# Splitting the last weight group, aggregating the statistics ahead, and sharing the output between two engines at the end of a hybrid decoder step

## The chip, the core and the metric

The kernel runs on one core of one Trainium2 chip. The metric is the device time of the program in microseconds (us), from its first to its last instruction, as the median of several runs. TensorE (PE in the profile) does the matmuls, VectorE (DVE), ScalarE (ACT) and GpSimd (POOL) the elementwise work. SyncE (SP), ACT and POOL also issue transfers between HBM and the on-chip memory (SBUF). Matmul results land in PSUM, in banks of 512 f32 numbers per partition.

## The reference

One layer of a hybrid decoder on 256 prompt tokens and 32 sample tokens (8 sequences of 4), 2048 features wide, all in f32. The change touches only the end of it, the feed-forward block and the layer norm behind it:

```python
merged = jax.nn.sigmoid(m_a) * y_a + jax.nn.sigmoid(m_b) * y_b
x = layer_norm(ALPHA * x + merged @ w_o, ln1_g, ln1_b)
hid = jnp.square(jax.nn.relu(x @ w_up))
x = layer_norm(ALPHA * x + hid @ w_down, ln2_g, ln2_b)
```

`w_down` is 8192 x 2048. `layer_norm` takes mean and variance over the 2048 features of a token, then scales by `g` and adds `b`.

## The kernel before, in words

**The stream.** All large weights go through one stream of blocks. A group (`add_group`, L151) is 256 output columns by some depth; a block is 4 row tiles of 128 by 256 columns, 512 KB. For block i, SP loads it (`load`, L164), ACT rounds it to a reduced f32 form (`split_hi`, L173), DVE takes the remainder (`split_lo`, L179), and PE multiplies (`matmuls`, L186): for each row tile and each half of 128 columns three matmuls, high times high, high times low, low times high (L202 to L204), 24 in a block, with the output feature on the partitions and the 288 tokens in the free dimension.

**Order of the work.** The order is written out by hand; every engine runs its queue in that order. Iteration i of the main loop (L1287) issues in turn `split_hi(i+3)`, `split_lo(i+3)`, the functions that are due at i, `matmuls(i)` and `load(i+7)`. What is due is what a group's `evac` list puts there: its functions run at the iterations after the group's last block (L207 to L209). The weight buffers are four deep, so ACT's `split_hi(i+3)` waits until PE is done with block i-1.

**The last quarter of `w_down`.** `w_down` is taken in four quarters of depth (c = 0 to 3), each in 8 groups p of 256 columns, added to the residual `acc` (feature-major, 16 tiles k of 128 features by 288 tokens; `down_evac`, L524). In the last quarter each finished group also starts the layer norm: `out_tiles(p)` (L580), three iterations later, turns its two tiles to token-major with four PE transposes (L591; two blocks b of 128 prompt tokens), DVE takes the statistics from PSUM (L594) and writes the tile times `ln2_g` to `Y` (L140 inside `scaled`, L596). For odd p, ACT copies the sample tokens of four tiles into `cs` (L604), and a generator, returned and run one iteration later by `rest` (L535), turns that copy with one more transpose (L608) and takes its statistics (L610). `tail_rows` (L571) prepares rows of `ln2_g` and `ln2_b` in `m5` for later. The last group (p = 7) is taken up after the stream has ended.

**The end (`final`, L620).** DVE merges the records of all 16 tiles for each token block (L627), ACT takes the root (L628), small operations make the mean and the factor of every token into `R`, PE turns `R` (L637), ACT copies it to `st5` (L638). The output of 8 units (token block b, 512 features n) is `Y * rs + rank1`, where `rank1` is a matmul of `st5` with `m5` (L650); unit 0 has it from DVE instead. All 8 units are DVE operations from PSUM, each followed by a store from SP (L688). Between them runs the sample's chain: merged moments (L656), a mean over four partitions by matmul (L660), copied by ACT (L661), the variance likewise (L668, L669), then ACT scales `gs` (L674), POOL adds `bs` (L675), DVE forms `Ys`, and ACT issues its four stores (L681).

**Buffers.** PSUM holds two accumulators of two banks (`acp`) and four banks (`gp`) that `gtile` hands out.

Of the kernel before, what the change touches and what calls it, by code (L numbers as in the profile page):

```python
# [16 lines left out]
P = 128  # L17
# [21 lines left out]


def _constants():
# [31 lines left out]
    f["rowhi"] = np.isin(k, (0, 2, 3)) * 1.0  # L73
# [30 lines left out]
def hybrid_kernel(ctx: ExitStack, tc: tile.TileContext, A):  # L104
# [46 lines left out]
    def add_group(W, col0, row0, nk, acts, evac, width=NT):  # L151
        gi = dict(W=W, col0=col0, acts=acts, evac=evac, width=width)
        for j in range(nk // KB):
            blocks.append((gi, row0 + j * KB * P, j * KB, j == 0, j == nk // KB - 1))
# [9 lines left out]
    def load(i):  # L164
        if i >= len(blocks):
            return
        gi, r0, k0, _, _ = blocks[i]
        t = wp.tile([P, KB, GW], F32, tag="raw", name=nm("raw"))
        sp.dma_start(t, gi["W"][r0:r0 + KB * P, gi["col0"]:gi["col0"] + GW]
                     .rearrange("(k p) c -> p k c", p=P))  # L170
        raw[i] = t
# [14 lines left out]
    def matmuls(i):  # L186
# [7 lines left out]
        for k in range(KB):  # L194
            for t in range(2):
# [5 lines left out]
                en = last and k == KB - 1  # L201
                pe.matmul(o, wh, xh_, start=st, stop=False)  # L202
                pe.matmul(o, wh, xl_, start=False, stop=False)  # L203
                pe.matmul(o, wl, xh_, start=False, stop=en)  # L204
                if fill:
                    fill.pop(0)()
# [317 lines left out]
    def down_evac(c, p):  # L524
# [3 lines left out]
        if c == 3:  # L528
            if p == 0:
                return [f, lambda ps: None, lambda ps: out_tiles(p, ps)]  # L530
            if p == 7:
                return [lambda ps: out_tiles(p, ps)]
# [8 lines left out]
            return [f, lambda ps: None, lambda ps: hold.extend(filter(None, [out_tiles(p, ps)])), rest]  # L541
        return [f]

    def tail_consts():
# [4 lines left out]
        gps.dma_start(ph["g2"], A["ln2_g"].to_broadcast([P, D]))  # L549
        gps.dma_start(ph["b0"], A["ln2_b"][:, 0:512].to_broadcast([P, 512]))  # L550
# [7 lines left out]
    def tail_tiles():  # L558
        pl = ph["pool"]
        g4 = pl.tile([P, D + 256], F32R, tag="R4", name="g4")  # L560
        ph["m5"], ph["st5"] = g4[0:5, 0:D], g4[0:5, D:D + 256]
# [5 lines left out]
        ph["sm"] = r5[:, 4320:4352]  # L567
        sp.dma_start(r5[0:3, 0:D], A["ln2_g"].to_broadcast([3, D]))
        sp.dma_start(r5[3:5, 0:D], A["ln2_b"].to_broadcast([2, D]))

    def tail_rows(n):  # L571
        c = slice(512 * n, 512 * n + 512)
        r5, m5 = ph["r5"], ph["m5"][:, c]
        raw_, lo = r5[0:5, 0, c], r5[0:5, 1, 1536:2048]
        act.copy(m5, raw_)
        tt(lo, raw_, m5, SUB)
        dve.tensor_scalar(out=m5, in0=m5, scalar1=cst("rowhi")[0:5, 0:1], scalar2=None, op0=MUL)
        stt(m5, lo, cst("rowlo")[0:5, 0:1], m5, MUL, ADD)

    def out_tiles(p, ps):  # L580
        if p == 0:
            ph["Y"] = ap_.tile([P, 2, D], F32, tag="ao", name="Y")
        Y, Ys, bn = ph["Y"], ph["Ys"], ph["bn"]
        a = ph["acc"]
        gv = [gtile()[:, 0:256].rearrange("p (b c) -> p b c", b=2) for _ in range(2)]
        if p == 7:
            for u in range(2):
                tt(a[:, 14 + u, :], a[:, 14 + u, :], ps[:, u, 0:NT], ADD)
        for u in range(2):
            for b in range(2):  # L590
                pe.transpose(gv[u][:, b, :], a[:, 2 * p + u, b * P:(b + 1) * P], ident)  # L591
        for u in range(2):
            for b in range(2):
                dve.bn_stats(out=bn[:, b, 2 * p + u, :], in_=gv[u][:, b, :])  # L594

        def scaled():  # L596
            for u in range(2):
                c = slice(256 * p + P * u, 256 * p + P * u + P)
                tt(Y[:, :, c], gv[u], bmid(ph["g2"][:, c], 2), MUL)

        w = p // 2
        if p % 2:
            cs = ph["cs"][:, (w % 2) * P:(w % 2) * P + P]
            act.copy(cs.rearrange("p (k t) -> p k t", k=4), a[:, 4 * w:4 * w + 4, NP_:NT])  # L604

        def sample():
            g2 = gtile()[:, 0:P]
            pe.transpose(g2, cs, ident)  # L608
            yield
            dve.bn_stats(out=ph["bns"][:, w, :], in_=g2)  # L610
            tt(Ys[:, w * P:(w + 1) * P], g2, ph["gs"][:, w * P:(w + 1) * P], MUL)
        if p == 7:
            ph["rest"] = scaled, sample()
            next(ph["rest"][1])
        else:
            scaled()
            if p % 2:
                return sample()

    def final():  # L620
        Y, Ys, bn, sm = ph["Y"], ph["Ys"], ph["bn"], ph["sm"]
        scaled, sample = ph["rest"]
        mv = sm[:, 0:4].rearrange("p (b s) -> p b s", b=2)
        sd, rs, r = sm[:, 4:6], sm[:, 6:8], sm[:, 8:10]
        R = ph["pool"].tile([P, 2, 5], F32R, tag="mv", name="R")
        for b in range(2):
            dve.bn_aggr(out=mv[:, b, :], in_=bn[:, b])  # L627
        act.activation(sd, mv[:, :, 1], AF.Sqrt, bias=epsc[:, 0:1])  # L628
        act.copy(R[:, :, 3:5], bc(ones[:, 0:2], 2))
        scaled()  # L630
        dve.reciprocal(out=rs, in_=sd)
        stt(r, mv[:, :, 0], -1.0, rs, MUL, MUL)
        stt(R[:, :, 0:2], bc(mv[:, :, 0], 2), -1.0, bc(rs, 2), MUL, MUL)
        tt(R[:, :, 2], r, R[:, :, 0], SUB)
        pr = gtile()
        for b in range(2):
            pe.transpose(pr[0:5, b * P:(b + 1) * P], R[:, b, :].bitcast(F32), ident)  # L637
        act.copy(ph["st5"], pr[0:5, 0:256])  # L638
# [3 lines left out]
        stt(t0, ph["g2"][:, 0:512], r[:, 0:1], ph["b0"], MUL, ADD)  # L642
        units = [(b, n) for b in range(2) for n in range(4)]
        rank1 = {0: t0}

        def prepare(i):
            if i < 8:
                b, n = units[i]
                rank1[i] = gtile()
                pe.matmul(rank1[i], ph["st5"][:, b * P:(b + 1) * P], ph["m5"][:, 512 * n:512 * n + 512],  # L650
                          start=True, stop=True)

        # sample: four rows of the tile hold a token
        def moments():
            next(sample, None)
            dve.bn_aggr(out=mq, in_=ph["bns"])  # L656

        def mean():
            pq = gtile()
            pe.matmul(pq[:, 0:2], cst("quart"), mq, start=True, stop=True)  # L660
            act.copy(me, pq[:, 0:2])  # L661

        def deviation():
            tt(dv, mq[:, 0:1], me[:, 0:1], SUB)
            tt(dv, dv, dv, MUL)
            tt(vb, me[:, 1:2], epsc[:, 0:1], ADD)
            pq = gtile()
            pe.matmul(pq[:, 0:1], cst("quart"), dv, start=True, stop=True)  # L668
            act.activation(ds, pq[:, 0:1], AF.Sqrt, bias=vb)  # L669

        def scale():
            dve.reciprocal(out=qs, in_=ds)
            stt(ts, me[:, 0:1], -1.0, qs, MUL, MUL)
            act.mul(ph["gs"], ph["gs"], ts)  # L674
            gps.tensor_tensor(out=ph["gs"], in0=ph["gs"], in1=ph["bs"], op=ADD)  # L675

        def finish():
            stt(Ys, Ys, qs, ph["gs"], MUL, ADD)
            ys = A["y_sample"].rearrange("b t (k j f) -> (b t) k j f", j=4, f=P)
            for j in range(4):  # L680
                act.dma_start(ys[:, :, j, :], Ys[32 * j:32 * j + 32, :].rearrange("p (k f) -> p k f", k=4))  # L681

        steps = {0: moments, 1: mean, 2: deviation, 4: scale, 7: finish}
        prepare(1)
        for i, (b, n) in enumerate(units):
            c = slice(512 * n, 512 * n + 512)
            stt(Y[:, b, c], Y[:, b, c], rs[:, b:b + 1], rank1[i], MUL, ADD)
            sp.dma_start(A["y_prompt"][0, b * P:(b + 1) * P, c], Y[:, b, c])  # L688
            prepare(i + 2)
            if i in steps:  # L690
                steps[i]()

    mark["up"] = len(blocks)
    for c in range(4):
# [4 lines left out]
        for p in range(8):  # L699
            add_group(A["w_down"][0], GW * p, 2048 * c, KT, lambda: (ph["hh"], ph["hl"]), down_evac(c, p))  # L700

# [149 lines left out]
    def gdn(G):  # L851
# [29 lines left out]
        # token-major keys; squared norms of keys and queries  # L881
# [490 lines left out]
```

## Time and profile before

| | |
|---|---|
| median of 3 runs | 1725.3 us (1725.29 to 1725.32) |
| the profiled execution, first to last instruction | 1725.5 us |
| PE busy | 1701.8 us (99%) |
| PE weight loads busy | 1677.6 us (97%) |
| DVE busy | 1026.3 us (59%) |
| ACT busy | 712.0 us (41%) |
| POOL busy | 123.7 us (7%) |
| mean granted TensorE clock | 0.991 of full speed |

A timeline row gives the start in us from the span's start, the length in us, the engine, the source line, the operation, what it writes and reads, shapes and count; in brackets stands how long the engine had been idle and what released it. PEld is PE's weight load, which overlaps matmuls. An engine with a q (ACTq, SPq) is that engine's queue issuing transfers. Rows merge neighbours of one kind ("x4"), so a row's length then covers all of them.

### The profile page before, as it was taken

Reading aid. Unit: us, or ns where it says so; the run is one execution under the profiler, and the core shown is the slowest. Engines: PE = TensorE matmul, PEld = TensorE weight load, DVE = VectorE, ACT = ScalarE, POOL = GpSimd, SP = SyncE. Lnnn points to the kernel's source line nnn. Section 1 sums busy time; section 2 is a strip of 40 time slices with the busy share of each in tenths; the row PEclk is TensorE's granted clock in tenths of the full one; section 3 lists DMA queues with packets and bytes.
Section 4 is the critical chain, followed back from the end, with each engine's and each line's share of the span. In section 5 each row is a group of like instructions: output and inputs, shape, how many; then the busy total and the mean of one; then the engine's idle time right before and its main releaser. Section 6 shows DMA issues by size and latency. Waiting matters only on the chain.

```text
span 1725.5 us, 31070 instructions
## 1 busy us (share of the span) xinstructions
PE 1701.8 (99%) x13037; PEld 1677.6 (97%) x13037; DVE 1026.3 (59%) x1345; ACT 712.0 (41%) x1031; POOL 123.7 (7%) x217
## 2 busy tenths in 40 slices
PE   9999999999999999999999999999999999999997
PEld 7999889999999999999999999999999999999996
DVE  5687777577454445545778754565445654456565
ACT  4664445334443333434445433344333433344331
POOL 2221231023300000000010000000000000000000
PEclk8999999999999999999999999999999999999998
DMA  8464347435655555555575555555555555555552
GB/s 241 141 181 137 106 118 233 131 103 151 207 169 162 169 165 166 159 171 160 170 204 164 166 168 163 168 160 167 166 167 163 159 171 166 165 164 166 163 158 78
DMA packets 272296, 279.76 MB, mean 162 GB/s; under 512 B 12122, under 2 KB 267035, under 8 KB 272023
## 3 DMA queue, kind: packets, MB, share of 16 engines
q1 hardware_dynamic: 267324, 265.87, 51.7%
q0 software_dynamic: 4256, 11.65, 2.3%
q8 instruction: 102, 1.67, 0.4%
q10 hardware_dynamic: 576, 0.26, 0.1%
q14 instruction: 38, 0.31, 0.0%
HBM read 270.26 MB, written 7.48 MB: 161 GB/s over the span
## 4 chain that ended last, share of the span: by engine, by line
issue 48%; PE 47%; DVE 2%; DMA 1%; ACT 1%; SPq 0%; POOLq 0%; POOL 0%; ACTq 0%; DVEq 0%
PE acc L202 14%; PE acc L203 14%; PE acc L204 14%; PE g L986 1%; DMA g<-in_ln_b_dram 1%; PE g L995 1%; DVE w L143 1%; DMA xr<-in_x_prompt_dram 0%; ACT hi L177 0%; DVE lo L140 0%; DVE w L266 0%; PE g L769 0%; DVE w L327 0%; PE g L1169 0%; PE g L1149 0%
## 5 line engine op out<-in xcount | busy, mean ns | idle before, releaser
L140 DVE TENSOR_TENSOR lo<-raw,hi 128x1024 fp32r<-128x1024 f32 (+2 forms) x502 | 608.0, 1214 | 551.6 <-ACT hi L177 549.1
L177 ACT CAST hi<-raw 128x1024 fp32r<-128x1024 f32 (+1 forms) x498 | 517.7, 1041 | 793.3 <-PE acc L203 729.7
L202 PE MATMUL acc<-xh,hi 128*128 128x288 f32 x1408 | 423.8, 301 | 0.0
L204 PE MATMUL acc<-xh,lo 128*128 128x288 f32 x1408 | 418.0, 297 | 0.0
L203 PE MATMUL acc<-xl,hi 128*128 128x288 f32 x1408 | 417.9, 297 | 0.0
L202 PE MATMUL acc<-dh,hi 128*128 128x290 f32 x1024 | 303.9, 297 | 0.0
L203 PE MATMUL acc<-dl,hi 128*128 128x290 f32 x1024 | 303.2, 296 | 0.0
L204 PE MATMUL acc<-dh,lo 128*128 128x290 f32 x1024 | 302.8, 296 | 0.0
L204 PE MATMUL acc<-hh,lo 128*128 128x288 f32 x1024 | 302.3, 295 | 0.0
L203 PE MATMUL acc<-hl,hi 128*128 128x288 f32 x1024 | 302.3, 295 | 0.0
L202 PE MATMUL acc<-hh,hi 128*128 128x288 f32 x1024 | 302.1, 295 | 0.0
L202 PEld LDWEIGHTS acc<-xh,hi 128*128 128x128 f32 x1408 | 266.8, 189 | 4.0 <-issue 1.6
L203 PEld LDWEIGHTS acc<-xl,hi 128*128 128x128 f32 x1408 | 266.9, 190 | 0.7
L204 PEld LDWEIGHTS acc<-xh,lo 128*128 128x128 f32 x1408 | 266.8, 189 | 0.0
L202 PEld LDWEIGHTS acc<-dh,hi 128*128 128x128 f32 x1024 | 193.6, 189 | 0.1
L204 PEld LDWEIGHTS acc<-dh,lo 128*128 128x128 f32 x1024 | 193.3, 189 | 0.0
L203 PEld LDWEIGHTS acc<-dl,hi 128*128 128x128 f32 x1024 | 193.2, 189 | 0.1
L203 PEld LDWEIGHTS acc<-hl,hi 128*128 128x128 f32 x1024 | 192.5, 188 | 0.0
L204 PEld LDWEIGHTS acc<-hh,lo 128*128 128x128 f32 x1024 | 192.3, 188 | 0.0
L202 PEld LDWEIGHTS acc<-hh,hi 128*128 128x128 f32 x1024 | 192.1, 188 | 0.0
L203 PE MATMUL acc<-ml,hi 128*128 128x288 f32 x256 | 75.6, 295 | 0.0
L204 PE MATMUL acc<-mh,lo 128*128 128x288 f32 x256 | 75.6, 295 | 0.0
(385 smaller groups left out, 1625.1 us busy)
## 6 DMA issues: line engine op xcount, KB each, us to landing
raw<-in_w_in_dram SPq DMA_DIRECT2D x176, 512.0 KB, 3.7
raw<-in_w_up_dram SPq DMA_DIRECT2D x128, 512.0 KB, 3.7
raw<-in_w_down_dram SPq DMA_DIRECT2D x128, 512.0 KB, 3.6
raw<-in_w_o_dram SPq DMA_DIRECT2D x32, 512.0 KB, 3.6
raw<-in_w_a_out_dram SPq DMA_DIRECT2D x16, 512.0 KB, 3.6
raw<-in_w_b_out_dram SPq DMA_DIRECT2D x16, 512.0 KB, 3.6
S<-in_state_gdn_dram POOLq DMA_DIRECT2D x8, 512.0 KB, 8.1
out_dram<-S POOLq DMA_DIRECT2D x8, 512.0 KB, 5.5
```

The costliest lines, as they stand in the source:

```text
L140: dve.tensor_tensor(out=out, in0=a, in1=b, op=op)
L143: dve.scalar_tensor_tensor(out=out, in0=a, scalar=s, in1=b, op0=o0, op1=o1)
L177: act.copy(his[i][:, k:k + step], raw[i][:, k:k + step])
L202: pe.matmul(o, wh, xh_, start=st, stop=False)
L203: pe.matmul(o, wh, xl_, start=False, stop=False)
L204: pe.matmul(o, wl, xh_, start=False, stop=en)
L986: pe.matmul(o, kqm[:, 64 * b:64 * b + 64], S0[:, hh, b, :], start=(b == 0), stop=(b == 7))
L995: pe.matmul(out[r, q * 64:q * 64 + 64], a[r, q, :], b[r, q, :], start=True, stop=True)
```

## The change

The last group of 256 columns becomes two groups of 128 columns, whose blocks are 8 row tiles deep (the same 512 KB and 24 matmuls a block). Tile 14 is added and turned while the last group still runs, and DVE merges the records of tiles 0 to 14 there (`collect`); the end merges only that result with the record of tile 15, in `fin`. For tiles 0 to 7, ACT multiplies `acc` by `ln2_g` in place (`act.mul` in `turned`, with `g2f`, a copy of `ln2_g` with one feature on each partition), and DVE no longer writes `Y` for them. At the end PE turns these eight scaled tiles again, straight into the two accumulators in PSUM (`wide`), and adds the rank part to them by matmul; ACT scales the sum by `rs` into `Y` (`act_unit`, four of the eight units), and SP stores 1024 columns at a time. Because the sum is scaled as a whole, the rank part of these units comes from a second set of rows, so `R` has twice the columns and six rows. The other four units stay on DVE. The sample's turning, `sample_tile`, is now started inside `out_tiles` at once and only its statistics wait for the next iteration. Its four stores are issued by ACT and SP, two each.

```diff
-    def add_group(W, col0, row0, nk, acts, evac, width=NT):
-        gi = dict(W=W, col0=col0, acts=acts, evac=evac, width=width)
+    def add_group(W, col0, row0, nk, acts, evac, width=NT, cols=GW):
+        kb = KB * GW // cols
+        gi = dict(W=W, col0=col0, acts=acts, evac=evac, width=width, cols=cols, kb=kb)
...
-            return [f, lambda ps: None, lambda ps: hold.extend(filter(None, [out_tiles(p, ps)])), rest]
+            return [f, lambda ps: None, lambda ps: hold.extend(filter(None, [out_tiles(p)])), rest]
...
+    def next_to_last(ps):
+        a = ph["acc"][:, 14, :]
+        tt(a, a, ps[:, 0, 0:NT], ADD)
+
+    def collect(ps):
+        turned(14)
+        fin, bn = ph["fin"], ph["bn"]
+        for b in range(2):
+            dve.bn_aggr(out=fin[:, b, 1:3], in_=bn[:, b, 0:15])
+        dve.tensor_scalar(out=fin[:, :, 2], in0=fin[:, :, 2], scalar1=15.0 * P, scalar2=None, op0=MUL)
...
+        sp.dma_start(ph["g2f"], A["ln2_g"][:, 0:1024].rearrange("o (k p) -> p (o k)", p=P))
...
+    def turned(k, record=None):
...
+        for b in range(2):
+            pe.transpose(gv[:, b, :], a[:, k, b * P:(b + 1) * P], ident)
+        for b in range(2):
+            dve.bn_stats(out=ph["bn"][:, b, k, :] if record is None else record[:, b], in_=gv[:, b, :])
...
+        if k >= 8:
+            scaled()
+        else:
+            act.mul(a[:, k, 0:NP_], a[:, k, 0:NP_], ph["g2f"][:, k:k + 1])
+
+    def sample_tile(w):
+        a = ph["acc"]
+        cs = ph["cs"][:, (w % 2) * P:(w % 2) * P + P]
+        act.copy(cs.rearrange("p (k t) -> p k t", k=4), a[:, 4 * w:4 * w + 4, NP_:NT])
+        g2 = gtile()[:, 0:P]
+        pe.transpose(g2, cs, ident)
+        yield
+        dve.bn_stats(out=ph["bns"][:, w, :], in_=g2)
+        if w == 3:
+            yield
+        tt(ph["Ys"][:, w * P:(w + 1) * P], g2, ph["gs"][:, w * P:(w + 1) * P], MUL)
+
+    def out_tiles(p):
+        for u in range(2):
+            turned(2 * p + u)
+        if p % 2:
+            g = sample_tile(p // 2)
+            next(g)
+            return g
+
+    def final(ps):
+        a, fin, sm = ph["acc"], ph["fin"], ph["sm"]
+        tt(a[:, 15, 0:NP_], a[:, 15, 0:NP_], ps[:, 0, 0:NP_], ADD)
+        tt(a[:, 15, NP_:NT], a[:, 15, NP_:NT], ps[:, 0, NP_:NT], ADD)
+        scaled = turned(15, fin[:, :, 3:9])
+        sample = sample_tile(3)
+        next(sample)
...
+        for b in range(2):
+            dve.bn_aggr(out=mv[:, b, :], in_=fin[:, b])
+        act.activation(sd, mv[:, :, 1], AF.Sqrt, bias=epsc[:, 0:1])
...
+        for n in range(2):
+            w = acp.tile([P, 2, 512], F32, tag="acc", name=nm("acc"))
+            wide.append(w)
+            for b in range(2):
+                for k in range(4):
+                    pe.matmul(w[:, b, P * k:P * k + P], a[:, 4 * n + k, b * P:(b + 1) * P], ident,
+                              start=(k == 0), stop=False, is_transpose=True)
...
+        act.copy(ph["st5"], pr[0:6, :])
...
+        def act_unit(b, n):
+            c = slice(512 * n, 512 * n + 512)
+            act.mul(Y[:, b, c], wide[n][:, b, :], rs[:, b:b + 1])
+            if n:
+                sp.dma_start(A["y_prompt"][0, b * P:(b + 1) * P, 0:1024], Y[:, b, 0:1024])
+
+        def dve_unit(b, n, rank1):
+            c = slice(512 * n, 512 * n + 512)
+            stt(Y[:, b, c], Y[:, b, c], rs[:, b:b + 1], rank1, MUL, ADD)
+            sp.dma_start(A["y_prompt"][0, b * P:(b + 1) * P, c], Y[:, b, c])
...
+        rank(wide[0][:, 0], 0, 0, 0, False)
+        r12 = rank_tile(1, 2)
+        pq = gtile()
+        pe.matmul(pq[:, 0:2], cst("quart"), mq, start=True, stop=True)
+        act.copy(me, pq[:, 0:2])
+        rank(wide[1][:, 0], 0, 0, 1, False)
+        act_unit(0, 0)
+        dve_unit(0, 2, t0)
+        next(sample, None)
+        tt(dv, mq[:, 0:1], me[:, 0:1], SUB)
+        tt(dv, dv, dv, MUL)
...
+        pe.matmul(pq2[:, 0:1], cst("quart"), dv, start=True, stop=True)
+        rank(wide[0][:, 1], 0, 1, 0, False)
+        rank(wide[1][:, 1], 0, 1, 1, False)
+        r03 = rank_tile(0, 3)
+        act.activation(ds, pq2[:, 0:1], AF.Sqrt, bias=vb)
+        dve_unit(1, 2, r12)
+        act_unit(0, 1)
+        dve.reciprocal(out=qs, in_=ds)
+        stt(ts, me[:, 0:1], -1.0, qs, MUL, MUL)
+        act.mul(ph["gs"], ph["gs"], ts)
+        gps.tensor_tensor(out=ph["gs"], in0=ph["gs"], in1=ph["bs"], op=ADD)
+        scaled()
+        act_unit(1, 0)
+        dve_unit(0, 3, r03)
+        r13 = rank_tile(1, 3)
+        dve_unit(1, 3, r13)
+        act_unit(1, 1)
+        stt(Ys, Ys, qs, ph["gs"], MUL, ADD)
...
+            (sp if j % 2 else act).dma_start(ys[:, :, j, :],
...
+        for p in range(8 if c < 3 else 7):
...
+    add_group(A["w_down"][0], D - 2 * P, 3 * 2048, KT, acts_h, [next_to_last, collect], cols=P)
+    add_group(A["w_down"][0], D - P, 3 * 2048, KT, acts_h, [final], cols=P)
```

More of the change, by code (lines that the diff above doesn't have):

```diff
@@ L606, in sample @@
[L606 to L622, printed above, removed]
+        a, Y = ph["acc"], ph["Y"]
@@ L626, in final @@
[L626 to L637, printed above, removed]
@@ L654, in moments @@
[L654 to L669, printed above, removed]
@@ L671, in scale @@
[L671 to L681, printed above, removed]
@@ L683, in final @@
-        steps = {0: moments, 1: mean, 2: deviation, 4: scale, 7: finish}
-        prepare(1)
-        for i, (b, n) in enumerate(units):
-            c = slice(512 * n, 512 * n + 512)
[L687 to L691, printed above, removed]
+        R = ph["pool"].tile([P, 2, 2, 6], F32R, tag="mv", name="R")
+        for b in range(2):
+            dve.bn_aggr(out=mv[:, b, :], in_=fin[:, b])
@@ new lines, in final @@
+        act.activation(sd, mv[:, :, 1], AF.Sqrt, bias=epsc[:, 0:1])
+        act.copy(R[:, 1, :, 3:5], bc(ones[:, 0:2], 2))
+        act.mul(R[:, 1, :, 5], ones[:, 0:2], 0.0)
+        m = mv[:, :, 0]
+        dve.tensor_scalar(out=R[:, 0, :, 0:2], in0=bc(m, 2), scalar1=-1.0, scalar2=None, op0=MUL)
+        stt(R[:, 0, :, 2], m, -1.0, R[:, 0, :, 0], MUL, SUB)
+        next(sample)
+        dve.reciprocal(out=rs, in_=sd)
+        act.copy(R[:, 0, :, 3:5], bc(sd, 2))
+        stt(r, m, -1.0, rs, MUL, MUL)
@@ new lines, in final, with rank @@
+        pr = gtile()
+        for s_ in range(2):
+            for b in range(2):
+                c = (2 * s_ + b) * P
+                pe.transpose(pr[0:6, c:c + P], R[:, s_, b, :].bitcast(F32), ident)
+        act.copy(ph["st5"], pr[0:6, :])
+        t0 = ph["r5"][:, 1, 1024:1536]
+        stt(t0, ph["g2"][:, 1024:1536], r[:, 0:1], ph["b0"], MUL, ADD)
+        def rank(out, s_, b, n, start):
+            c = (2 * s_ + b) * P
+            pe.matmul(out, ph["st5"][:, c:c + P], ph["m5"][:, 512 * n:512 * n + 512], start=start, stop=True)
```

99 lines of the change are left out of this document (47 added, 52 removed).

## The prediction

> **What bounds the kernel now.** I read the page first, then the timeline of the end, then that of the last quarter of `w_down`.
>
> ```profile
> span 1725.5 us, 31070 instructions
> PE 1701.8 (99%) x13037; PEld 1677.6 (97%) x13037; DVE 1026.3 (59%) x1345; ACT 712.0 (41%) x1031; POOL 123.7 (7%) x217
> ```
>
> PE is busy 99% of the span, so a wait put into its queue moves everything behind it. Only the end is not bound by PE. Its timeline, one engine at a time:
>
> ```profile
> 1708.46 0.82 DVE L140 TENSOR_TENSOR acc<-acc,acc 128x288 f32<-128x288 f32 x2 [5.04 <-PE acc L204]
> 1708.97 0.80 PE L591 MATMUL g<-cf,acc 128*128 128x128 f32 x4 [0.55 <-DVE acc L140]
> 1709.44 0.89 DVE L594 BATCH_NORM_STATS2 r<-g 128x6 f32<-128x128 f32 x4 [0.16 <-PE g L591]
> 1710.25 1.01 DVE L627 BATCH_NORM_AGGREGATE r<-r 128x2 f32<-128x96 f32 x2
> 1711.30 0.30 ACT L628 ACTIVATE r<-r,epsc 128x2 f32<-128x2 f32 x1 [1.69 <-DVE r L627]
> 1712.25 0.16 DVE L140 TENSOR_TENSOR R<-r,R 128x2 fp32r<-128x2 f32 x1
> 1712.55 0.38 PE L637 MATMUL g<-cf,R 128*5 128x128 f32 x2 [2.56 <-DVE R L140]
> 1712.97 0.36 ACT L638 CAST g<-g 5x256 fp32r<-5x256 f32 x1 [1.29 <-PE g L637]
> 1713.38 1.05 PE L650 MATMUL g<-g 5*128 5x512 f32 x3 [0.45 <-ACT g L638]
> 1714.17 0.25 DVE L656 BATCH_NORM_AGGREGATE r<-r 128x2 f32<-128x24 f32 x1
> 1715.10 0.16 ACT L661 COPY r<-g 128x2 f32<-128x2 f32 x1 [1.77 <-PE g L660]
> 1716.65 0.26 ACT L669 ACTIVATE r<-g,r 128x1 f32<-128x1 f32 x1 [1.39 <-PE g L668]
> 1717.62 0.72 ACT L674 ACTIVATE g<-g,r 128x512 f32<-128x512 f32 x1 [0.71 <-DVE r L143]
> 1718.43 1.26 POOL L675 TENSOR_TENSOR g<-g 128x512 f32<-128x512 f32 x1 [822.05 <-ACT g L674]
> 1719.73 0.75 DVE L143 SCALAR_TENSOR_TENSOR r<-r,g 128x512 f32<-128x512 f32 x1 [0.16 <-POOL g L675]
> 1720.51 2.65 ACTq L681 DMA_DIRECT2D out_dram<-r  x4
> ```
>
> The stream ends at 1708.46, and 17.0 us follow. The sample's chain ends last: its sums wait behind the prompt's statistics (R ready at 1712.41), then ACT, POOL and DVE follow each other to 1720.48, and four store issues of 0.66 us end at 1723.2.
>
> **Part 1: PE waits put into the stream.** In the order to which the changed kernel is built, the sample's transpose stands, for p = 1, 3 and 5, directly behind the four transposes of `out_tiles`; it reads ACT's copy `cs`. Before, it stood a block later. ACT's queue ahead of that copy holds `split_hi`, and for p = 1 and 3 now also two in-place scalings of 128x256. Behind the waiting transpose is all of PE's stream.
>
> ```profile
> 1635.08 0.49 PEld L591 LDWEIGHTS g<-cf,acc 128*128 128x128 f32 x4
> 1635.54 0.19 PEld L202 LDWEIGHTS acc<-hh,hi 128*128 128x128 f32 x1
> 1691.65 0.14 PEld L608 LDWEIGHTS g<-cf,r 128*128 128x128 f32 x1
> 1635.28 1.05 ACT L177 CAST hi<-raw 128x1024 fp32r<-128x1024 f32 x1 [2.14 <-PE acc L203]
> 1636.24 0.29 ACT L604 COPY r<-acc 128x128 f32<-128x128 f32 x1
> 1661.75 1.05 ACT L177 CAST hi<-raw 128x1024 fp32r<-128x1024 f32 x1 [2.14 <-PE acc L203]
> 1662.71 0.29 ACT L604 COPY r<-acc 128x128 f32<-128x128 f32 x1
> 1688.23 1.05 ACT L177 CAST hi<-raw 128x1024 fp32r<-128x1024 f32 x1 [2.14 <-PE acc L203]
> 1689.18 0.29 ACT L604 COPY r<-acc 128x128 f32<-128x128 f32 x1
> L514 ACT ACTIVATE r<-r,w 128x288 f32<-128x288 f32 x16 | 7.7, 528 | 20.1 <-DVE r L143 20.1
> ```
>
> PE is through its four transposes at 1635.54, 0.26 us after ACT began `split_hi`; that cast itself waits for PE's last block, so ACT cannot run ahead. p = 5: the copy ends at 1689.18 + 0.29 = 1689.47, the hand-over takes 0.05 (ACT L638 ends at 1713.33, PE's L650 starts at 1713.38), and PE would have gone on at 1688.23 + 0.26 = 1688.49: it waits 1.03 us. p = 1 and 3: no row has the scaling. It lies between the 5x256 cast, 0.36, and the 128x288 activation, 0.53; I take 0.50, the nearer row in operation and width. Neighbours on ACT overlap by 0.09 (the cast of 1.05 at 1635.28 is followed at 1636.24), so two cost 0.82 (0.54 to 0.88). The copy then ends at 1636.24 + 0.82 + 0.29 = 1637.35, PE goes on at 1637.40: 1.86 us late. p = 3 likewise: 1662.71 + 0.82 + 0.29 + 0.05 - 1662.01 = 1.86. The sum is 1.03 + 1.86 + 1.86 = 4.75 us (4.2 to 4.9). The transpose itself (0.14) was in the stream before as well. Tile 14's two transposes come into it from the end: 2 x 0.115 (0.46 for four) = 0.23. **The stream ends 5.0 us later** (4.4 to 5.2).
>
> The rest of the stream I cost at nothing. The blocks of 128 columns have the same bytes and matmuls, DVE's sums for tile 14 lie beside the last block. Their shorter rows and the small load of `g2f` ahead of the weights on SP are covered by the weights loaded four blocks ahead (a block is some 3.3 us); a late block would cost no more than its own delay.
>
> **Part 2: the end.** Times count from the first addition (1708.46 before).
> - The addition of 256 columns takes about 0.42, the hand-over and two transposes 0.52 (1708.97 to 1709.44, and the 0.05 ahead), two statistics 0.42. Two merges of 9 numbers instead of 96: 0.25 for 24 and 0.5 for 96 give 0.19 each. The moments are there at 1.7 instead of 2.8.
> - R: six small DVE operations of 0.16 with their hand-overs, the root of 0.30 and the sample's statistics, about 1.1: ready at 2.8. PE meanwhile does 16 transposes for `wide`, 16 x 0.115 = 1.84, begun at 1.06 behind the sample's transpose: 2.9. So R is turned at 2.95 instead of 4.06 (1712.52). Four transposes 0.61, the copy of 6x512 some 0.61 instead of 0.36, two rank matmuls of 0.34 instead of three, and the mean's matmul: ACT's copy of the mean starts at about 5.55 instead of 6.64.
> - ACT's root of the variance: DVE no longer has a 0.7 us unit in the way, 6.85 instead of 8.19. ACT puts one unit of 0.72 ahead of the scaling of `gs`: 7.65 instead of 9.16. POOL 1.26 and DVE 0.75 follow as before: `Ys` is ready at 10.5 instead of 12.02, 1.5 us earlier. Two issues instead of four on each queue save 2 x 0.66 = 1.3. Together 2.8 us, if nothing else ends last.
> - The stores of `Y` come closer together:
>
> ```profile
> 1716.00:1717.00 1.00, 1.00 (x4) 0.82 (x4) 1.00 (x3) 0.26 (x1) 0.00 (x0) 0.50 1.02 383
> L688 SPq DMA_DIRECT2D out_dram<-Y x8: 332/332/366, 1713.9 to 1719.6; - x8
> DMA to landing us min/median/max: 2.3/2.3/2.5
> DMA to landing us min/median/max: 2.1/2.1/2.2
> ```
>
> At 383 GB/s the transfer engines are full (1.02). ACT's unit (0,1) releases 512 KB at 7.75, DVE 2 x 256 KB at 8.8 and 9.5, ACT again 512 KB at 9.7, the sample 256 KB at 10.5: 1.8 MB behind 8.6 (0.87 from issue to data), at 0.37 MB per us until 13.5, and landed at 14.1, against 13.3 for the sample alone and 16.16 before. That leaves 2.0. **I take 2.2 us of gain** (1.5 to 2.9, the two ends last).
>
> **The sum.** 1725.5 + 5.0 - 2.2 = 1728.3 in the profiled execution's terms. It spans 0.2 more than the median of the runs (1725.3), so 1728.1.
>
> **Rivals.**
>
> (B) *PE's clock falls in the new waits: slower.* Granted clock by windows of the trace, and matmuls of the stream at full and at half clock:
>
> ```profile
> 229.30:232.72 3.42, 1.52 (x9) 0.87 (x7) 3.24 (x10) 1.48 (x3) 0.00 (x0) 1.00 0.20 71
> 232.72:239.55 6.83, 6.68 (x27) 6.27 (x26) 4.82 (x9) 0.38 (x2) 3.03 (x2) 0.50 0.37 92
> 1707.26:1710.68 3.42, 2.18 (x14) 1.46 (x12) 2.06 (x7) 0.30 (x1) 0.00 (x0) 1.00 0.00 0
> 228.74 0.29 PE L202 MATMUL acc<-xh,hi 128*128 128x288 f32 x1
> 229.14 0.30 PE L202 MATMUL acc<-xh,hi 128*128 128x288 f32 x1
> 235.22 0.44 PE L202 MATMUL acc<-xh,hi 128*128 128x288 f32 x1
> 235.94 0.44 PE L202 MATMUL acc<-xh,hi 128*128 128x288 f32 x1
> ```
>
> The trace's changes of the clock lie on one grid of 3.4133 us (232.72 and 239.55 are two steps apart). In the window that ends at 232.72 PE was busy 1.52 of 3.42 us, and the clock then was 0.50 for 6.83 us; with 2.18 busy it was not cut. At half clock three matmuls take 0.72 instead of 0.40, so a cut costs 6.83 x (1 - 0.40/0.72) = 3.0 us. The grid's window 1635.60 to 1639.02 (411 steps behind 232.72) would hold the whole wait of p = 1 (matmuls out at 1635.81, on at 1637.40: 1.59 idle), which leaves 1.83 busy: between 1.52 and 2.18, so the trace does not decide. With the grid at the same place p = 3's wait also falls into one window, so both are cut or none: 1728.1 + 6.0 = 1734.1. It decides from somewhere between 1.52 and 2.18 us of busy time. For the forecast: most of that rest is dense stream, while the cut window held a few scattered small matmuls.
> The Trainium skill, TensorE: Matmul & The Clock Gate, section "Why this matters for your kernels", asks only that PE-idle gaps stay under about 3 us. By that rule the waits cost no clock and the time stays 1728.1. This trace speaks against it: the longest gap in the cut window was 1.7 us.
>
> (C) *Only one of the two waits is cut* (the grid lies elsewhere): 1731.1.
>
> (D) *The change doesn't put PE into these waits*, because ACT is ahead of PE by the length of a cast: no row shows that, ACT's casts start only when PE's block is through (2.14 idle until PE). Then 1725.3 + 0.2 - 2.2 = 1723.3, at best 1722.6.
>
> **How the numbers follow.** Forecast 0.60, B 0.25, C 0.08, D 0.04, unforeseen 0.03. About 0.2% (3.45 us) is what a measurement of this kernel can tell from no change: 1721.9 to 1728.8. Of the forecast's own range, 1725.3 + 4.4 - 2.9 = 1726.8 to 1725.3 + 5.2 - 1.5 = 1729.0, about four fifths lie within it. Same: 0.48 + 0.04 = 0.52; slower: 0.12 + 0.25 + 0.08 = 0.45; faster: 0.03. Without B the range would leave out over 2 in 10, so it reaches from 1726.5 to 1734.5.
>
> **What would show it.** PE idle rows ahead of the sample's transpose at p = 1, 3 and 5, released by ACT's copy, of 1.9, 1.9 and 1.0 us; the first addition of tile 15 at about 1713.5 in a full-speed stream and near 1719.5 with two cuts; from there to the span's end 14.8 us instead of 17.0. It is wrong if these waits are missing, if the granted clock is 0.50 behind them, or if another chain than the stores and `Ys` ends last.

## The result and the profile after

| | before | after |
|---|---|---|
| median of 20 runs each, taken in turn | 1725.17 us (1723.87 to 1725.89) | 1727.93 us (1727.38 to 1728.53) |
| after / before | | 1.0017, 95% interval 1.0010 to 1.0023 |
| profiled execution, first to last instruction | 1725.5 us | 1726.7 us |

The change costs 2.8 us. The two profiled executions cannot be subtracted from each other as they stand: they differ by 1.75 us in the first part of the program, which the change does not touch (before p = 1 the same transposes of `out_tiles` begin at 1635.08 before and 1633.34 after). So I count from those transposes: 90.5 us to the end before, 93.4 after, +2.9, which agrees with the medians.

The page of the changed kernel, first lines of part 1:

```profile
span 1726.7 us, 31122 instructions
PE 1702.6 (99%) x13055; PEld 1678.2 (97%) x13055; DVE 1022.5 (59%) x1340; ACT 718.3 (42%) x1045; POOL 125.5 (7%) x218
```

Nothing is to be seen here: 4.6 us of idle PE are 0.3% of the span. The timeline shows them. PE's weight loads at p = 1, 3 and 5 (the sample's transpose, L623), and ACT's queue ahead of the first:

```profile
1635.63 0.14 PEld L623 LDWEIGHTS g<-cf,r 128*128 128x128 f32 x1 [1.80 <-ACT r L621]
1663.89 0.14 PEld L623 LDWEIGHTS g<-cf,r 128*128 128x128 f32 x1 [1.80 <-ACT r L621]
1691.36 0.14 PEld L623 LDWEIGHTS g<-cf,r 128*128 128x128 f32 x1 [1.00 <-ACT r L621]
1633.54 1.05 ACT L179 CAST hi<-raw 128x1024 fp32r<-128x1024 f32 x1 [2.14 <-PE acc L207]
1634.49 0.90 ACT L616 ACTIVATE acc<-acc,r 128x256 f32<-128x256 f32 x2
1635.30 0.28 ACT L621 COPY r<-acc 128x128 f32<-128x128 f32 x1
```

The brackets are to be read: PE's loader stood still for 1.80 us until ACT's copy L621 released it. The three add up to 4.60 us. The ACT rows show why: a cast of 1.05, two scalings of together 0.90, then the copy.

The end, counted in the text from the first addition (1711.52):

```profile
1709.07 0.97 DVE L554 BATCH_NORM_AGGREGATE r<-r 128x2 f32<-128x90 f32 x2
1711.52 0.52 DVE L140 TENSOR_TENSOR acc<-acc,acc 128x256 f32<-128x256 f32 x2 [1.27 <-PE acc L208]
1712.60 1.91 PE L675 MATMUL acc<-cf,acc 128*128 128x128 f32 x16
1712.89 0.32 DVE L653 BATCH_NORM_AGGREGATE r<-r 128x2 f32<-128x9 f32 x2
1714.18 0.23 DVE L140 TENSOR_TENSOR R<-r,R 128x2 fp32r<-128x2 f32 x2
1714.47 0.60 PE L681 MATMUL g<-cf,R 128*6 128x128 f32 x4
1716.80 0.16 ACT L710 COPY r<-g 128x2 f32<-128x2 f32 x1 [1.12 <-PE g L709]
1717.40 0.38 PE L719 MATMUL g<-r,g 128*128 128x1 f32 x2 [0.21 <-DVE r L140]
1717.82 0.26 ACT L723 ACTIVATE r<-g,r 128x1 f32<-128x1 f32 x1 [0.28 <-PE g L719]
1718.48 0.69 ACT L692 ACTIVATE Y<-acc,r 128x512 f32<-128x512 f32 x1 [0.39 <-PE acc L688]
1719.06 0.71 ACT L728 ACTIVATE g<-g,r 128x512 f32<-128x512 f32 x1
1719.86 1.26 POOL L729 TENSOR_TENSOR g<-g 128x512 f32<-128x512 f32 x1 [118.49 <-ACT g L728]
1721.16 0.75 DVE L143 SCALAR_TENSOR_TENSOR r<-r,g 128x512 f32<-128x512 f32 x1 [0.84 <-POOL g L729]
1721.93 1.57 SPq L739 DMA_DIRECT2D out_dram<-r  x2
1721.94 1.62 ACTq L739 DMA_DIRECT2D out_dram<-r  x2
```

The merge of tiles 0 to 14 (128x90) is over before the last addition; behind it two merges of 9 numbers are left, 0.32 us. `Ys` is ready at 1721.91, 10.4 us behind the addition. The last stored byte landed at 1725.56 (14.04 us), the program ended 1.16 later: 15.2 us, against 17.08 before. So the end gained 1.9 us and the stream lost 4.8 (from the transposes of p = 1 to the first addition: 78.18 us, before 73.38).

The windows of the transfers (last two columns: share of the 16 engines, GB/s), and issue to landing:

```profile
1720.00:1722.00 2.00, 0.00 (x0) 0.00 (x0) 1.07 (x2) 0.93 (x2) 1.12 (x1) 0.50 1.00 389
1722.00:1724.00 2.00, 0.00 (x0) 0.00 (x0) 0.00 (x0) 0.00 (x0) 0.00 (x0) 0.50 1.05 395
out_dram<-Y SPq DMA_DIRECT2D x2, 512.0 KB, 3.2
out_dram<-r SPq DMA_DIRECT2D x2, 64.0 KB, 2.8
```

For four microseconds the transfer engines are full, and the sample's stores land 2.8 us after their issue instead of 2.1.

The granted clock is the column ahead of the last two. The two windows of the grid that hold the waits of p = 1 and p = 3, and the two that follow them:

```profile
1633.80:1637.21 3.41, 1.85 (x15) 1.61 (x14) 2.03 (x5) 1.78 (x4) 0.00 (x0) 1.00 0.52 169
1661.11:1664.52 3.41, 1.85 (x15) 1.61 (x15) 1.64 (x4) 2.04 (x4) 0.00 (x0) 1.00 0.50 154
1637.21:1640.62 3.41, 3.41 (x28) 3.41 (x27) 0.44 (x1) 1.52 (x2) 0.00 (x0) 1.00 0.40 136
1664.52:1667.93 3.41, 3.41 (x28) 3.41 (x27) 0.39 (x2) 0.57 (x1) 0.00 (x0) 1.00 0.52 156
```

PE was busy for 1.85 of 3.41 us in both, and the clock behind them stayed at 1.00.

### The profile page after: what moved, and what is told of

Same layout as the page of the kernel before. It is cut to its first block, busy times and chain, and to the rows that moved or that the text cites. A ratio compares the mean times of both kernels' runs of the same rounds, so it can differ in the third digit from the quotient of the medians.

```text
span 1726.7 us, 31122 instructions
## 1 busy us (share of the span) xinstructions
PE 1702.6 (99%) x13055; PEld 1678.2 (97%) x13055; DVE 1022.5 (59%) x1340; ACT 718.3 (42%) x1045; POOL 125.5 (7%) x218
## 4 chain that ended last, share of the span: by engine, by line
PE 53%; issue 43%; DVE 2%; ACT 1%; DMA 0%; POOL 0%; SPq 0%; POOLq 0%; ACTq 0%; DVEq 0%
PE acc L206 16%; PE acc L207 16%; PE acc L208 16%; PE g L1039 1%; PE g L1048 1%; DVE w L143 1%; ACT hi L179 1%; DVE lo L140 0%; DMA xr<-in_x_prompt_dram 0%; PE g L822 0%; DVE w L270 0%; DVE w L331 0%; PE g L1222 0%; PE g L1202 0%; PE g L1225 0%
```

## The experiments

The theory: three waits of PE for ACT's copy cost the stream 4.6 us, and the end gives back about 2. Rivals: the stream loses its time in something else of the change (the blocks of 128 columns, tile 14, the scalings); or the waits are harmless in themselves and the time goes through the clock. e1 to e4 deal with the stream, e5 to e10 with the end. All times below are medians; each has the ratio to the kernel before, run beside it, whose median lay between 1724.99 and 1725.21.

### e1: the sample's transpose a block later again

In `sample_tile`, for all but the last four tiles:

```diff
         act.copy(cs.rearrange("p (k t) -> p k t", k=4), a[:, 4 * w:4 * w + 4, NP_:NT])
+        if w < 3:
+            yield
         g2 = gtile()[:, 0:P]
```

> The changed kernel, with the sample's transpose for p = 1, 3 and 5 put back one iteration behind ACT's copy. Theory (the change's loss is the time PE waits for that copy, its gain is at the end): the three waits of 1.8, 1.8 and 1.0 us go, 4.6 us less than the changed kernel's 1727.9, so 1723.3; 1.9 us under the kernel before. Rival (the waits are taken up elsewhere in the stream, and the end is what became slower): the time stays at 1727 to 1728.

Measured 1723.62 us (1722.62 to 1724.27, 11 runs), ratio 0.9989 (0.9980 to 0.9998): 4.3 us less than the changed kernel, and faster than both. PE's weight loads at p = 1, of the four transposes and of the sample's:

```profile
1632.81 0.49 PEld L604 LDWEIGHTS g<-cf,acc 128*128 128x128 f32 x4
1636.42 0.14 PEld L625 LDWEIGHTS g<-cf,r 128*128 128x128 f32 x1
```

The sample's transpose stands a block (3.6 us) behind the others, with no bracket: PE did not wait. From these transposes to the first addition the stream takes 73.62 us against 73.38 before; the 0.24 left over are about what the prediction took for tile 14's two transposes (0.23). So nothing else of the change costs the stream time worth naming, and the first rival falls.

### e2: that move alone, in the kernel before

```diff
-                return sample()
+                g = sample()
+                next(g)
+                return g
```

> The kernel before, with that transpose alone put directly behind the four transposes of out_tiles, nothing else changed. Theory: three waits of 1.0 us each (ACT's cast and the copy, no scalings), so 3.0 us over the kernel before, 1728.2, without any of the gain at the end. Rival (PE's stream takes up a wait of 1 us): no difference from the kernel before.

Measured 1728.89 us (1726.90 to 1730.77, 11 runs), ratio 1.0019 (1.0010 to 1.0028). The same transposes now carry the wait:

```profile
1634.33 0.14 PEld L608 LDWEIGHTS g<-cf,r 128*128 128x128 f32 x1 [1.00 <-ACT r L604]
1661.79 0.14 PEld L608 LDWEIGHTS g<-cf,r 128*128 128x128 f32 x1 [1.00 <-ACT r L604]
1689.25 0.14 PEld L608 LDWEIGHTS g<-cf,r 128*128 128x128 f32 x1 [1.00 <-ACT r L604]
```

3 x 1.00 without the scalings. From the transposes of p = 1 (1632.84) to the first addition (1709.17) the stream takes 76.3 us, 3.0 more than in the kernel before. The median rose by 3.7; 0.4 of the rest is the end, which in this profile took 17.49 us (below, on the clock), and the last 0.3 lie within the interval of the ratio (1.7 to 4.8 us).

### e3: the copy ahead of the scalings

The changed kernel with e1's edit, and the copy is issued first, the transpose directly behind the four others as in the change:

```diff
     def out_tiles(p):
+        g = sample_tile(p // 2) if p % 2 else None
+        if g:
+            next(g)
         for u in range(2):
             turned(2 * p + u)
-        if p % 2:
-            g = sample_tile(p // 2)
+        if g:
             next(g)
```

> The changed kernel, with ACT's copy for the sample put ahead of the two in-place scalings; the transpose stays where the change put it. Theory: PE then waits 1.0 us at p = 1 and 3 as at p = 5, so 1.6 us less than the changed kernel, 1726.3. Rival (the scalings have no part in the wait): 1727.9 as before.

Measured 1726.39 us (1724.89 to 1728.87, 11 runs), ratio 1.0006 (0.9998 to 1.0015). The trace shows the copy directly behind the cast, the scalings behind the copy, and three waits of 1.00; the first:

```profile
1634.29 0.29 ACT L621 COPY r<-acc 128x128 f32<-128x128 f32 x1
1634.63 0.14 PEld L625 LDWEIGHTS g<-cf,r 128*128 128x128 f32 x1 [1.00 <-ACT r L621]
```

From the transposes of p = 1 (1633.14) to the first addition (1709.72) the stream takes 76.6 us, 1.6 less than in the changed kernel. So the wait of 1.80 is 1.00 for the cast and the copy and 0.80 for the two scalings, as the prediction had it.

### e4: a longer wait, for the clock

The changed kernel with one more copy of 128x512 on ACT (its result is not used) ahead of the sample's at p = 1 and 3:

```diff
         if p % 2:
+            if p < 5:
+                act.copy(ph["r5"][:, 1, 1024:1536], ph["g2"][:, 1024:1536])
             g = sample_tile(p // 2)
```

> The changed kernel, with one more ACT copy of 128x512, read by nobody, ahead of the sample's copy at p = 1 and 3. The wait grows by about 0.53 us each time, and PE would be busy about 1.3 us in a clock window that holds all of it (1.83 in the changed kernel, 1.52 in the one window whose clock was cut before). If the clock goes by PE's busy time in such a window with its bound between 1.52 and 1.83: two cuts of 3.0 us and 1.1 us of waiting, 1735. If waits as short as these cost no clock, as the rule of 3 us says: 1.1 us over the changed kernel, 1729.0.

Measured 1732.21 us (1730.82 to 1733.18, 4 runs), ratio 1.0039 (1.0026 to 1.0053): between the two numbers expected. The wait at p = 1, and the windows of the grid that hold it and follow it:

```profile
1635.28 0.14 PEld L623 LDWEIGHTS g<-cf,r 128*128 128x128 f32 x1 [2.32 <-ACT r L621]
```

```profile
1632.15:1635.56 3.41, 1.33 (x11) 1.09 (x10) 1.81 (x5) 2.56 (x5) 0.00 (x0) 1.00 0.49 154
1635.57:1638.98 3.41, 3.41 (x17) 3.41 (x16) 0.21 (x2) 0.00 (x0) 0.00 (x0) 0.50 0.48 154
1638.99:1642.40 3.41, 3.41 (x27) 3.41 (x27) 1.04 (x1) 1.57 (x2) 0.00 (x0) 1.00 0.00 0
```

Here the mechanism of rival B is at work: 1.33 us busy out of 3.41, and the next window runs at 0.50. But it is one window, not the two (6.83 us) of the cut at 232.72 in the kernel before. At the prediction's spacing (three matmuls in 0.72 instead of 0.40 us) such a window loses 3.41 x (1 - 0.40/0.72) = 1.5 us. p = 3 shows the same. The stream agrees: from the transposes of p = 1 (1632.47) to the first addition (1714.75) it takes 82.3 us, 4.1 more than in the changed kernel, 2 x 0.52 for the longer waits and 2 x 1.5 for the cuts. 1727.9 + 4.1 = 1732.0, and the clock's earlier fall at the end of the profiled execution (below) adds 0.45: 1732.5, against 1732.2 measured. So for a wait like this one the bound lies between 1.33 and 1.85 us of busy time, and the change was on the safe side of it by less than 0.52 us a window. It is not a bound on busy time in general: in e4's own trace a window with 2.15 us busy elsewhere in the program (229.28 to 232.70) is followed by 0.50.

The Trainium skill (TensorE: Matmul & The Clock Gate, section "Why this matters for your kernels") asks for no idle gap of PE over some 3 us between bursts, as one window of idle time brings the half clock back. The changed kernel's waits of 1.80 agree with that; here waits of 2.32 cut the clock both times, and the measurement decides. The same page, section "What's actually happening", gives a free-running window of 3413 ns, and the grid of these traces agrees (3.41 us from 1635.57 to 1638.99).

### e5: four small stores in place of two wide ones

The kernel of e1; each of ACT's units is stored by itself:

```diff
-            if n:
-                sp.dma_start(A["y_prompt"][0, b * P:(b + 1) * P, 0:1024], Y[:, b, 0:1024])
+            sp.dma_start(A["y_prompt"][0, b * P:(b + 1) * P, c], Y[:, b, c])
```

> The end of the kernel with the deferred transpose (e1, 1723.6 us), but each of ACT's four units is stored by itself (256 KB each) instead of two stores of 512 KB. Unit (0,0) can then leave some 1.6 us earlier, and behind ACT's last unit 256 KB remain instead of 512. Theory (the full transfer engines end last): 256 KB less in the last stretch at about 0.39 MB per us is 0.65 us less, 1723.0. Rival (the sample's chain and its issues end last): no gain, and the two added issues of some 0.6 us on SP may put its first store of the sample off by 0.2: 1723.6 to 1723.8.

Measured 1724.28 us (1723.46 to 1725.36, 11 runs), ratio 0.9996 (0.9987 to 1.0005): 0.7 more than e1, not less. In the trace the last landing is at 14.71 us behind the first addition (e1: 14.10). Both theories missed SP's queue. Its rows:

```profile
1711.73 0.37 SPq L695 DMA_DIRECT2D out_dram<-Y  x1
1712.15 0.92 SPq L700 DMA_DIRECT2D out_dram<-Y  x2
```

The first store is ACT's unit (0,0), 6.1 us behind the first addition (1705.66). DVE's unit (0,2), ready 1.6 us earlier, stands behind it in program order, and waits. e9 mends that.

### e9: the same in order of readiness

```diff
-        act_unit(0, 0)
         dve_unit(0, 2, t0)
+        act_unit(0, 0)
```

> The kernel with four stores of 512 columns for ACT's units (e5), with one edit: DVE's unit (0,2) is issued ahead of ACT's (0,0), so that SP does not hold the ready store of (0,2) for 1.6 us behind that of (0,0). Theory (the order on SP's queue cost e5 what the smaller stores should have gained): the first store leaves 4.5 us behind the first addition as in e1, the sample's last store lands between 13.55 (as in e6, with hardly any other transfer) and e1's 14.10, I take 13.7, and the time is about 1723.2. Rival (stores of 512 columns move slower, 0.35 instead of 0.39 MB per us, and that cost e5 its time): landing at 14.4 or later, 1724.0.

Measured 1723.97 us (1723.51 to 1726.43, 11 runs), ratio 0.9997 (0.9988 to 1.0006); last landing at 15.13. The first store now leaves at 4.5, as expected, but `Ys` was ready only at 11.08 instead of 10.39, because in this execution the clock fell earlier (below). From `Ys` to the last landing, which the clock does not touch, e9 takes 4.05 us, e5 4.3, e1 3.7. So the smaller stores do not gain even in good order. The windows of 1.5 us in which the transfer engines were full behind ACT's last unit, e1 first, e9 second:

```profile
1717.43:1718.93 1.50, 0.00 (x0) 0.00 (x0) 0.00 (x0) 0.00 (x0) 0.00 (x0) 0.50 1.06 400
```

```profile
1717.84:1719.34 1.50, 0.00 (x0) 0.00 (x0) 0.09 (x1) 0.00 (x0) 0.00 (x0) 0.50 1.05 348
1719.34:1720.84 1.50, 0.00 (x0) 0.00 (x0) 0.00 (x0) 0.00 (x0) 0.00 (x0) 0.50 1.02 319
```

Equally full engines move 400 GB/s in e1's window, and 319 to 348 here; by these rates, and by a landing that would be at 14.4 without the clock's 0.7, the rival is the better account. Its reason, the stores of 512 columns as such, is not shown. The kernel before stores all of `y_prompt` in the same rows of 2 KB and moved 383 GB/s at a share of 1.02 (the window from 1716.00 in the prediction). Nor is it the sample's small pieces: in e5 a window in which none of them moved yet is the slowest of all:

```profile
1716.66:1718.16 1.50, 0.00 (x0) 0.00 (x0) 0.00 (x0) 0.00 (x0) 0.00 (x0) 0.50 1.09 313
```

What slows the transfers there stays open. The Trainium skill (Perfetto Trace Analysis, section "DMA Optimizations") advises both larger pieces, 4 KB rather than 2, and splitting where the engines are idle, so that some start sooner; here 400 GB/s in e1 against 383 in the kernel before is what the size of the rows can have brought at most, and for splitting the condition, idle engines, is not met where the share is above 1.

### e6: without the wide stores

```diff
-            if n:
-                sp.dma_start(A["y_prompt"][0, b * P:(b + 1) * P, 0:1024], Y[:, b, 0:1024])
```

> The kernel with the deferred transpose (e1, 1723.6 us) without the two stores of 1024 columns, so the first half of y_prompt is not written. All other work stands. Theory (the transfer engines are full at the end): the sample's stores then land 2.1 us after their issue as in the kernel before, instead of 2.6 to 3.2, so 0.5 to 1.1 us less, about 1722.9. Rival (their landing takes that long by itself, from the two queues or the small pieces): 1723.6, landing unchanged.

Measured 1723.46 us (1721.78 to 1724.14, 11 runs), ratio 0.9988 (0.9979 to 0.9997): by the runs no difference from e1 that could be told. In the trace `Ys` is ready at the same time (10.38) and the last landing comes at 13.55 instead of 14.10. The landing of the sample's stores:

```profile
out_dram<-r SPq DMA_DIRECT2D x2, 64.0 KB, 2.1
```

2.1 us as in the kernel before, against 3.1 in e1 (2.8 in the changed kernel, above). So the full transfer engines cost 0.55 us at the end, at the lower edge of what was expected.

### e7: all eight units on DVE

The kernel of e1 with the eight DVE units of the kernel before, `R` of six columns, no second turning of tiles 0 to 7 and no in-place scaling; the merge ahead and the two queues stay:

```diff
-        if k >= 8:
-            scaled()
-        else:
-            act.mul(a[:, k, 0:NP_], a[:, k, 0:NP_], ph["g2f"][:, k:k + 1])
+        scaled()
...
-            act.mul(Y[:, b, c], wide[n][:, b, :], rs[:, b:b + 1])
...
+            stt(Y[:, b, c], Y[:, b, c], rs[:, b:b + 1], rank1[i], MUL, ADD)
```

> The kernel with the deferred transpose (e1, 1723.6 us) with all eight units of the output on DVE as before the change: no in-place scaling by ACT, no second turning into PSUM, no wide stores; the split last group, the statistics merged ahead and the sample's stores on two queues stay. Theory (most of the 1.9 us gained at the end come from the moments being 1.1 us earlier and from the two queues; ACT's half brings only what DVE's eight units delay Ys by): Ys at about 11.0 us behind the first addition instead of 10.4, about 0.5 us more than e1: 1724.1. Rival (ACT's half is what gains): the end is as long as in the kernel before, 1.9 us more than e1: 1725.5.

Measured 1723.99 us (1723.37 to 1725.48, 11 runs), ratio 0.9994 (0.9986 to 1.0003): 0.4 more than e1. The last three units and `Ys` on DVE, and POOL's addition:

```profile
1715.37 2.06 DVE L143 SCALAR_TENSOR_TENSOR Y<-Y,r,g 128x512 f32<-128x512 f32 x3
1715.64 1.26 POOL L698 TENSOR_TENSOR g<-g 128x512 f32<-128x512 f32 x1 [114.54 <-ACT g L697]
1717.35 0.75 DVE L143 SCALAR_TENSOR_TENSOR r<-r,g 128x512 f32<-128x512 f32 x1
```

`Ys` starts without a wait, right behind DVE's units, half a microsecond after POOL was through: DVE is the bound, and `Ys` is ready at 11.4 instead of 10.4. But its stores then land 3.16 us behind `Ys`, 3.71 in e1, and the last landing is at 14.55, 0.45 behind e1. The clock fell early in this execution, 5.4 us behind the first addition, which in e4 and e9 alone delayed `Ys` by 0.5 to 0.7 us (the table below). So what half of the output on ACT gives the sample's chain is at most 1.0 us and may be half of that; 0.55 of it goes to the fuller transfer engines again, and 0.45 at the end is an upper bound.

### e8: the sample's stores on one queue

```diff
-            (sp if j % 2 else act).dma_start(ys[:, :, j, :],
+            act.dma_start(ys[:, :, j, :],
```

> The kernel with the deferred transpose (e1, 1723.6 us) with all four stores of the sample issued by ACT as in the kernel before, instead of two each by ACT and SP. The fourth issue then ends some 1.2 us later. Theory (full transfer engines hold up the landing of the two-queue stores, so the later issue finds them empty): landing 2.1 us after issue instead of 2.6 to 3.2, a net loss of about 0.5: 1724.1. Rival (the issue alone sets the end): 1.3 more, 1724.9.

Measured 1724.28 us (1723.12 to 1726.23, 11 runs), ratio 0.9995 (0.9986 to 1.0004); last landing at 14.85, 0.75 later than e1 with `Ys` at the same 10.39. ACT's four issues:

```profile
1716.58 2.97 ACTq L741 DMA_DIRECT2D out_dram<-r  x4
```

They take 2.97 us, the two that ACT issues in e1 take 1.60, so the last ends 1.4 later; 0.75 of that reaches the end, between the 0.5 of the theory and the 1.3 of the rival: part of it falls into the time in which the engines are full anyway.

### e10: all statistics merged at the end

The kernel of e1 without the merge in `collect`:

```diff
-        for b in range(2):
-            dve.bn_aggr(out=fin[:, b, 1:3], in_=bn[:, b, 0:15])
-        dve.tensor_scalar(out=fin[:, :, 2], in0=fin[:, :, 2], scalar1=15.0 * P, scalar2=None, op0=MUL)
...
-            dve.bn_aggr(out=mv[:, b, :], in_=fin[:, b])
+            dve.bn_aggr(out=mv[:, b, :], in_=ph["bn"][:, b])
```

> The kernel with the deferred transpose (e1, 1723.6 us) with the statistics of all 16 tiles merged at the end, as before the change: two merges of 96 numbers (1.01 us) behind the last statistics instead of two of 9 (0.32). Theory (the merge stands in the sample's chain): R 0.7 us later, Ys at 11.0 to 11.1 instead of 10.39, and as the transfer engines are then less full at the end, 0.5 to 0.7 us more: 1724.2. Rival (the full transfer engines or PE's second turning end last, the merge ahead is hidden): 1723.6.

Measured 1723.88 us (1723.53 to 1725.36, 11 runs), ratio 0.9993 (0.9984 to 1.0002).

```profile
1707.19 1.02 DVE L651 BATCH_NORM_AGGREGATE r<-r 128x2 f32<-128x96 f32 x2
```

1.02 instead of 0.32: ACT's copy of the mean starts 0.7 later, at 5.98 instead of 5.28 behind the first addition, and nothing hides that. `Ys` came at 11.46 and the last landing at 15.12, 1.0 behind e1: the 0.7 of the merge, and 0.3 to 0.4 that I put to a clock that fell earlier in the chain (7.0 us behind the first addition, in a chain that is 0.7 later); no run separates the two.

By the medians of the runs, e5 to e10 lie within 0.8 us of e1, and each ratio is known to 0.0009 (1.5 us) either way. So the verdicts on them rest on the traces, not on the medians.

## Why the prediction was right

The forecast of 1728.1 us met the 1727.9 measured, in the case that it had put first. That it met to 0.2 us is in part luck: it had the stream 0.2 us and the gain at the end 0.3 us too large, and these cancel. That the clock would hold was a judgement, which the trace of before could not decide. Step by step:

**Part 1, PE's waits.** Right in mechanism, order and size: 1.86 + 1.86 + 1.03 = 4.75 forecast, 1.80 + 1.80 + 1.00 = 4.60 found. The scaling of 128x256, which no row of before showed, takes 0.90 for two overlapped instead of 0.82. e1 takes the waits away and with them 4.3 us; e2 puts them into the kernel before; e3 splits them into their two parts.

**Part 1, the rest at nothing.** Right: 0.24 us are left in e1's stream, as much as was forecast for the two transposes of tile 14 (0.23).

**Part 2, the chain.** Moments at 1.7 (1.69 found), `R` turned from 2.95 (2.95), mean copied at 5.55 (5.28), root at 6.85 (6.30), scaling of `gs` at 7.65 (7.54), `Ys` at 10.5 (10.4). The middle was forecast up to 0.55 too late, but ACT's unit ahead of the scaling then waited 0.39 us for PE's rank sum (`[0.39 <-PE acc L688]` in the timeline above), and most of that lead was gone.

**Part 2, the stores.** Right: landed at 14.1 forecast, 14.04 found, with the engines full at 389 to 395 GB/s; e6 shows that they, not the chain alone, hold the last landing up.

**Part 2, the gain.** The term that was mis-sized: 2.2 taken, 1.9 found. The step's own sum for the stores had given 2.0. The landing did come 2.1 us earlier, but from the last landing to the end the program takes 1.16 us instead of 0.92, which the sum had no term for. And one thing the step left out: the clock. In the profile of before it fell 5.6 us behind the first addition, within the sample's chain; in that of after 7.6 behind it. The same kind of matmul of the chain (128x1, two of them) took 0.59 before (L668) and 0.38 after (L719). The windows of the grid, before and then after:

```profile
1714.10:1717.51 3.41, 3.12 (x9) 2.06 (x8) 3.34 (x12) 0.42 (x2) 0.00 (x0) 0.50 0.61 231
```

```profile
1715.72:1719.13 3.41, 2.96 (x11) 1.73 (x11) 2.37 (x10) 1.66 (x5) 0.00 (x0) 1.00 0.25 96
```

How much that is worth the experiments show, since each fell at its own place of the grid (us behind the first addition, from the traces):

| kernel | clock falls | `Ys` ready | last landing | end |
|---|---|---|---|---|
| e2 (end as before) | 2.7 | 12.4 | 16.57 | 17.49 |
| before | 5.6 | 12.0 | 16.16 | 17.08 |
| e9 (see there) | 5.5 | 11.1 | 15.13 | 16.47 |
| e4 (end as after) | 6.2 | 10.9 | 14.49 | 15.65 |
| after | 7.6 | 10.4 | 14.04 | 15.20 |
| e1 | 7.6 | 10.4 | 14.10 | 15.08 |
| e3 (end as after) | 8.5 | 10.4 | 14.08 | 15.06 |

An early fall of the clock delays the changed end's `Ys` by 0.5 to 0.7 us. At about the same place of the fall (before 5.6, e4 6.2) the landing gains 16.16 - 14.49 = 1.7, not 2.1. How much of the 1.9 in the two profiles is luck of the grid can't be fixed more closely than that, since no run of the old end had a late fall; the medians (2.8 in all, 4.8 lost in the stream) say 2.0.

**The sum.** That the profiled execution "spans 0.2 more than the median" set two things side by side that differ in kind: the run that gave the profile of after has 1728.50 us as its time and 1726.7 from first to last instruction, 1.8 apart. The profiled execution of before was then about 2 us slower than the median, in the start. No harm came of it, as only differences were added.

**Rival B** (the clock cut in both waits, 1734.1) did not occur here; its mechanism did in e4. Two of its terms were off: with 1.85 us busy the clock held, and the cuts of e4, each followed by a full window, lasted 3.41 us, not 6.83, so each cost 1.5, not 3.0. **C** did not occur. **D**, no waits, would have given 1723.3; the kernel that really has none (e1) takes 1723.62.

**What the end's 1.9 us are made of.** Each part undone alone in e1 moves the last landing by: merge ahead 0.7 (e10, its clock taken off), two queues 0.75 (e8), ACT's half at most 0.45 (e7). The prediction had priced the first two, the moments at 1.1 together with the shorter additions and the issues at 1.3, and of ACT's half only the DVE unit that no longer stands in the sample's way. ACT's half, the largest part of the change, is the smallest of these gains. What the split of the last group gives, no run undoes alone; the merge at the end starts 1.36 us behind the first addition in e10 and 1.79 in the kernel before.

## What to carry to other kernels

On an engine that is busy 99% of the time, the place of a small operation in its queue is worth more than a rebuilt end: a transpose moved ahead by one block lost 4.6 us where the whole new ending gained about 2. Before moving such an operation, read in the timeline how far behind the engine that feeds it runs; here ACT starts its cast only when PE's block is through, so PE always meets it at work. With a yield of two lines (e1) the same change is faster than both kernels, 1723.6 us.

## What the runs showed of the hardware beyond that

- A cut of the clock lasted one grid window where PE was busy through all of it: 3.41 us, 1.5 us lost (e4, both times), and 3.41 us at 232.67 in e1. At 232.72 in the kernel before PE was busy for 3.26 of the first 3.41 us, and the cut lasted 6.83.
- Busy time alone does not decide the cut at the end of the program, where small transposes and matmuls with 6 rows run. A window of e9 with 2.75 us busy is followed by 0.50, one of after with 2.76 by 1.00. e9's with the window that follows, then that of after, whose next window is the one at 1.00 shown above (1715.72):

```profile
1708.88:1712.29 3.41, 2.75 (x18) 1.73 (x16) 2.50 (x11) 0.98 (x6) 0.00 (x0) 1.00 0.03 11
1712.31:1715.70 3.39, 2.86 (x7) 1.65 (x6) 2.48 (x9) 2.03 (x5) 0.00 (x0) 0.50 0.58 219
```

```profile
1712.31:1715.71 3.40, 2.76 (x23) 2.10 (x21) 3.06 (x15) 1.21 (x6) 0.00 (x0) 1.00 0.00 0
```

  What the chip counts there stays open.
- Two executions of nearly the same program differed by 1.75 us before the part that the change touches. The difference is there early: ACT's cast of the same block starts at 143.24 before and at 141.51 after. What made it is not shown.
- From the last landing to the last instruction passed 0.92 to 1.35 us, with no rule that these runs show.
